# A row softmax on one core: the first loads shared between two DMA queues

## The chip, the cores and the metric

The kernel runs on one core of one Trainium2 chip. The core has a vector engine (VectorE, "DVE" in the profile), a scalar engine (ScalarE, "ACT"), a GpSimd ("POOL") and a Sync engine ("SP") which here only issues DMA transfers. Data move between the device memory and the on-chip memory, which has 128 partitions, by 16 DMA engines. An instruction stream starts a transfer by issuing a DMA on its own queue: Sync's is q1 in the profile, ScalarE's is q10. The metric is the device time of one execution in microseconds (us).

## What is computed

A softmax over the last axis of a float32 array of 16 x 1024 x 512, with temperature 0.5:

```python
temp = 0.5
x_scaled = x / temp
x_max = np.max(x_scaled, axis=-1, keepdims=True)
exp_x = np.exp(x_scaled - x_max)
return (exp_x / np.sum(exp_x, axis=-1, keepdims=True)).astype(np.float32)
```

There are 16,384 rows of 512 numbers: 33.55 MB in and as much out.

## The kernel before

**Tiles.** The 16,384 rows are cut into eight tiles (`c` = 0 to 7). A tile has 128 partitions of `G` = 16 rows each, so 32 KB in a partition and 4.19 MB in all. The 16 rows of a partition follow one another in device memory, so one partition's share is one unbroken piece. Six buffers (`BUFS`) hold tiles 0 to 5; tile 6 takes over the buffer of tile 0, tile 7 that of tile 1, so their loads wait until the stores of tiles 0 and 1 are done.

**Loads.** `load(c)` issues a tile's load on Sync's queue (line 66), all 128 partitions at a time. Tile 0 comes in two parts, four rows of each partition (1 MB) and then twelve (3 MB); the others come whole. Sync has no other work: it runs through its nine issues in order and stops only where a buffer is not free.

**Blocks.** Computation goes by blocks: tile 0 has three (4, 4 and 8 rows of each partition), tiles 1 to 6 have one each, tile 7 has two of 8. So there are eleven blocks, and the loop index `i` counts them. Each passes through these steps, all in place in the tile's buffer:

- `shift(i)`: VectorE takes the negated maximum of each row (line 74, `negmax`) and doubles it (line 78, `bias`).
- `exponentials(i)`: ScalarE computes exp(2x + bias) row by row of each partition and the row's sum with it (line 85), 16 instructions for a full tile.
- `scale_vector(i)`: VectorE takes the reciprocals of the sums (line 100) and multiplies seven eighths of the rows by them (line 102).
- `scale_scalar(i)`: ScalarE multiplies the remaining rows (line 111).
- `store(i)`: at the last block of a tile ScalarE issues the store of the whole tile on its own queue (line 119).

**Order.** The order of instructions is written out by hand (`manual_schedule`), and every engine runs its own in that order. The loop is skewed: in round `i`, ScalarE does the exponentials of block `i+1` before it finishes block `i`, and VectorE scales block `i` and then takes the maximum of block `i+2`. A load is issued in `shift` when a tile is first needed by that order; as Sync waits for nothing but buffers, its first seven issues go out at the start. ScalarE's first instruction of use is a dummy exponential on one column (`warm`, line 52), which brings the load of its function table ahead of the first data.

Of the kernel before, what the change touches and what calls it, by code (L numbers as in the profile page):

```python
# [1 line left out]

# [4 lines left out]


@with_exitstack
def kernel(  # L10
    ctx: ExitStack,
    tc: tile.TileContext,
    x: bass.AP,
    out: bass.AP,
):
    nc = tc.nc
    fp32 = mybir.dt.float32
    P = nc.NUM_PARTITIONS
    AX = mybir.AxisListType.X
    EXP = mybir.ActivationFunctionType.Exp  # L20
    COPY = mybir.ActivationFunctionType.Copy
    MAX = mybir.AluOpType.max

    D = x.shape[-1]
    xf = x.flatten_outer_dims()
    of = out.flatten_outer_dims()
    N = xf.shape[0]

    G = 16
    C = N // (P * G)
    assert C * P * G == N
    xr = xf.rearrange("(c p g) d -> c p g d", p=P, g=G)
    outr = of.rearrange("(c p g) d -> c p g d", p=P, g=G)
    WHOLE = [(0, G)]
    LOADS = [[(0, 4), (4, G)]] + [WHOLE] * 7
    BLOCKS = [[(0, 4), (4, 8), (8, G)]] + [WHOLE] * 6 + [[(0, 8), (8, G)]]
    STORES = [WHOLE] * 8  # L40
    BMAX = 16
    BUFS = 6

    data = ctx.enter_context(tc.tile_pool(name="data", bufs=BUFS))
    stats = ctx.enter_context(tc.tile_pool(name="stats", bufs=6))

    ctx.enter_context(tc.manual_schedule())


    warm = stats.tile([P, 1], fp32, name="warm", bufs=1)  # L50
    nc.vector.memset(warm, 0.0)  # L51
    nc.scalar.activation(out=warm, in_=warm, func=EXP)  # L52

    chunks = {}
    blocks = [(c, lo, hi) for c in range(C) for lo, hi in BLOCKS[c]]
    n = len(blocks)
    biases, sums, recips = {}, {}, {}

    def load(c):
        if c < BUFS:  # L60
            chunks[c] = data.tile([P, G, D], fp32, name="xt")
        else:
            chunks[c] = chunks[c - BUFS]
        xt = chunks[c]
        for lo, hi in LOADS[c]:
            nc.sync.dma_start(out=xt[:, lo:hi, :], in_=xr[c][:, lo:hi, :])  # L66

    def shift(i):
        c, lo, hi = blocks[i]
        if c not in chunks:  # L70
            load(c)
        b = hi - lo
        negmax = stats.tile([P, BMAX], fp32, name="negmax")
        nc.vector.tensor_reduce(  # L74
            negmax[:, 0:b], chunks[c][:, lo:hi, :], axis=AX, op=MAX, negate=True
        )
        biases[i] = stats.tile([P, BMAX], fp32, name="bias")
        nc.vector.tensor_scalar_mul(biases[i][:, 0:b], negmax[:, 0:b], 2.0)  # L78

    def exponentials(i):  # L80
        c, lo, hi = blocks[i]
        sums[i] = stats.tile([P, BMAX], fp32, name="sums")
        for g in range(hi - lo):
            row = chunks[c][:, lo + g, :]
            nc.scalar.activation(  # L85
                out=row,
                in_=row,
                func=EXP,
                bias=biases[i][:, g : g + 1],
                scale=2.0,  # L90
                accum_out=sums[i][:, g : g + 1],
            )


    def scale_vector(i):
        c, lo, hi = blocks[i]
        b = hi - lo
        k = b - b // 8
        recips[i] = stats.tile([P, BMAX], fp32, name="recip")
        nc.vector.reciprocal(recips[i][:, 0:b], sums[i][:, 0:b])  # L100
        rows = chunks[c][:, lo : lo + k, :]
        nc.vector.tensor_mul(  # L102
            rows, rows, recips[i][:, 0:k].unsqueeze(2).broadcast_to((P, k, D))
        )

    def scale_scalar(i):
        c, lo, hi = blocks[i]
        b = hi - lo
        for g in range(b - b // 8, b):
            row = chunks[c][:, lo + g, :]  # L110
            nc.scalar.activation(  # L111
                out=row, in_=row, func=COPY, scale=recips[i][:, g : g + 1]
            )

    def store(i):
        c, _, end = blocks[i]
        for lo, hi in STORES[c]:
            if hi == end:
                nc.scalar.dma_start(
                    out=outr[c][:, lo:hi, :], in_=chunks[c][:, lo:hi, :]  # L120
                )

    shift(0)
    shift(1)
    exponentials(0)
    for i in range(n):
        if i + 1 < n:
            exponentials(i + 1)
        scale_vector(i)
        scale_scalar(i)  # L130
        if i + 2 < n:
            shift(i + 2)
        store(i)


# [1 line left out]
_INS = ['x']  # L137
_OUTS = [((16, 1024, 512), 'float32')]


# [23 lines left out]
```

## Time and profile before

| | |
|---|---|
| Median of three runs | 162.38 us (162.26 to 162.4) |
| The profiled execution's own time | 162.34 us |
| Its span in the profile | 160.6 us |
| Reads and writes of device memory | 33.55 MB and 33.55 MB, 418 GB/s over the span |
| Waits of ScalarE for VectorE's `bias` | 41.2 us in 10 waits, the longest 5.9 |
| Median time of a store from issue to landing | 22.8 us |
| Median time of a whole tile's load from issue to landing | 30.2 us |

The profile's span starts and ends a little inside the device time; 1.74 us lie around it here. A row of the timeline gives the start and the duration in us, the engine, the line of the kernel, the operation, and what it writes and reads with its shape; in brackets stands how long the engine was idle before it and what ended that. "SPq" and "ACTq" are the instructions with which Sync and ScalarE issue transfers. A row of the waits gives who waited for what, the total in us, how often, and the longest. A DMA queue's row gives packets, megabytes, and the time of its packets as a share of 16 engines' span. A row of the windows gives the stretch, its length, the busy time of VectorE, ScalarE and GpSimd in it (with the number of instructions), TensorE's granted clock, the DMA engines' busy share and the GB/s moved.

### The profile page before, as it was taken

Reading aid. Unit: us, or ns where it says so; the run is one execution under the profiler, and the core shown is the slowest. Engines: PE = TensorE matmul, PEld = TensorE weight load, DVE = VectorE, ACT = ScalarE, POOL = GpSimd, SP = SyncE. Lnnn points to the kernel's source line nnn. Section 1 sums busy time; section 2 is a strip of 40 time slices with the busy share of each in tenths; the row PEclk is TensorE's granted clock in tenths of the full one; section 3 lists DMA queues with packets and bytes.
Section 4 is the critical chain, followed back from the end, with each engine's and each line's share of the span. In section 5 each row is a group of like instructions: output and inputs, shape, how many; then the busy total and the mean of one; then the engine's idle time right before and its main releaser. Section 6 shows DMA issues by size and latency. Waiting matters only on the chain.

```text
span 160.6 us, 402 instructions
## 1 busy us (share of the span) xinstructions
DVE 134.6 (84%) x45; ACT 102.1 (64%) x273; POOL 0.2 (0%) x4
## 2 busy tenths in 40 slices
DVE  0507999999999999999999999999999999957000
ACT  3071549069979963998199909991899891790000
POOL 0000000000000000000000000000000000000000
DMA  5999999999999999999999999999999999999993
GB/s 182 471 400 506 400 400 498 408 392 484 424 400 384 400 457 449 400 441 465 400 424 473 408 408 492 400 392 498 416 392 490 424 392 457 457 392 449 465 392 139
DMA packets 2450, 67.13 MB, mean 418 GB/s; under 512 B 272, under 2 KB 272, under 8 KB 272
## 3 DMA queue, kind: packets, MB, share of 16 engines
q1 hardware_dynamic: 1296, 33.56, 49.3%
q10 hardware_dynamic: 1152, 33.55, 48.4%
q14 instruction: 2, 0.02, 0.0%
HBM read 33.55 MB, written 33.55 MB: 418 GB/s over the span
## 4 chain that ended last, share of the span: by engine, by line
DVE 80%; DMA 7%; ACT 4%; issue 0%; SPq 0%
DVE negmax L74 42%; DVE xt L102 36%; DMA xt<-in_x_dram 7%; ACT xt L85 4%; DVE bias L78 1%; DVE recip L100 1%; SPq L66 0%
## 5 line engine op out<-in xcount | busy, mean ns | idle before, releaser
L85 ACT ACTIVATE xt<-xt,bias 128x512 f32<-128x512 f32 x128 | 90.4, 708 | 41.7 <-DVE bias L78 41.2
L74 DVE TENSOR_REDUCE negmax<-xt 128x16 f32<-128x8192 f32 (+2 forms) x11 | 69.9, 6352 | 9.5 <-DMA xt<-in_x_dram 9.5
L102 DVE TENSOR_TENSOR xt<-xt,recip 128x7168 f32<-128x7168 f32 (+2 forms) x11 | 62.0, 5637 | 0.4
L85 ACT ACTIVATION_READ_ACCUMULATOR xt<-xt,bias 128x1 f32 x128 | 23.9, 187 | 0.0
L111 ACT ACTIVATE xt<-xt,recip 128x512 f32<-128x512 f32 x15 | 9.9, 706 | 0.0
L100 DVE RECIPROCAL recip<-sums 128x16 f32<-128x16 f32 (+2 forms) x11 | 2.4, 218 | 1.8 <-ACT xt L85 1.8
L78 DVE TENSOR_SCALAR bias<-negmax 128x16 f32<-128x16 f32 (+2 forms) x11 | 1.9, 173 | 0.4
L52 ACT ACT_TABLE_LOAD x1 | 1.3, 1283 | 0.7 <-PEq L148 0.7
L51 DVE MEMSET warm<- 128x1 f32 x1 | 0.1, 59 | 0.8 <-PEq L148 0.8
L52 ACT ACTIVATE warm<-warm 128x1 f32<-128x1 f32 x1 | 0.2, 203 | 0.0
L148 POOL MEMSET const-bfloat16-1.0<- 128x1 bf16 x1 | 0.1, 103 | 0.0
L148 POOL MEMSET const-uint8-127<- 128x1 uint8 x1 | 0.1, 103 | 0.0
L148 POOL MEMSET const-float32-1.0<- 128x1 f32 x1 | 0.1, 100 | 0.0
L148 POOL MEMSET const-float32-0.0<- 128x1 f32 x1 | 0.1, 99 | 0.2 <-issue 0.2
## 6 DMA issues: line engine op xcount, KB each, us to landing
out_dram<-xt ACTq DMA_DIRECT2D x8, 4096.0 KB, 22.8
xt<-in_x_dram SPq DMA_DIRECT2D x7, 4096.0 KB, 30.2
xt<-in_x_dram SPq DMA_DIRECT2D x1, 3072.0 KB, 11.7
xt<-in_x_dram SPq DMA_DIRECT2D x1, 1024.0 KB, 4.9
```

Source lines behind the costliest of these rows:

```text
L51: nc.vector.memset(warm, 0.0)
L52: nc.scalar.activation(out=warm, in_=warm, func=EXP)
L74: nc.vector.tensor_reduce(negmax[:, 0:b], chunks[c][:, lo:hi, :], axis=AX, op=MAX, negate=True)
L78: nc.vector.tensor_scalar_mul(biases[i][:, 0:b], negmax[:, 0:b], 2.0)
L85: nc.scalar.activation(out=row, in_=row, func=EXP, bias=biases[i][:, g : g + 1], scale=2.0, accum_out=sums[i][:, g : g + 1],)
L100: nc.vector.reciprocal(recips[i][:, 0:b], sums[i][:, 0:b])
L102: nc.vector.tensor_mul(rows, rows, recips[i][:, 0:k].unsqueeze(2).broadcast_to((P, k, D)))
L111: nc.scalar.activation(out=row, in_=row, func=COPY, scale=recips[i][:, g : g + 1])
L148: nc = _bacc.Bacc("TRN2", target_bir_lowering=False, num_devices=1)
```

## The change

Tiles 0, 1 and 2 (`SHARED` = 3) are loaded in two transfers each (tile 0 in two for each of its parts): partitions 0 to 63 on Sync's queue, partitions 64 to 127 on ScalarE's. Tile 3 is loaded whole on ScalarE's queue. Tiles 4 to 7 stay on Sync's queue, whole. The loads of tiles 0 to 2 are issued before anything else; the dummy exponential with its table load comes after them in ScalarE's order. The loads of tiles 3, 4 and 5 are issued after the exponentials of the first block: on ScalarE this places tile 3's load behind those four instructions, while Sync, which has none of them, goes on to tiles 4 and 5 at once. The stores stay on ScalarE's queue, now behind these loads. No computation changes.

```diff
+    SHARED = 3
+
     data = ctx.enter_context(tc.tile_pool(name="data", bufs=BUFS))
     stats = ctx.enter_context(tc.tile_pool(name="stats", bufs=6))
 
     ctx.enter_context(tc.manual_schedule())
-
-
-    warm = stats.tile([P, 1], fp32, name="warm", bufs=1)
-    nc.vector.memset(warm, 0.0)
-    nc.scalar.activation(out=warm, in_=warm, func=EXP)
...
         for lo, hi in LOADS[c]:
-            nc.sync.dma_start(out=xt[:, lo:hi, :], in_=xr[c][:, lo:hi, :])
+            halves = [(nc.sync, 0, P)]
+            if c == SHARED:
+                halves = [(nc.scalar, 0, P)]
+            if c < SHARED:
+                halves = [(nc.sync, 0, P // 2), (nc.scalar, P // 2, P)]
+            for queue, p, q in halves:
+                queue.dma_start(out=xt[p:q, lo:hi, :], in_=xr[c][p:q, lo:hi, :])
...
+    for c in range(SHARED):
+        load(c)
+
+
+    warm = stats.tile([P, 1], fp32, name="warm", bufs=1)
+    nc.vector.memset(warm, 0.0)
+    nc.scalar.activation(out=warm, in_=warm, func=EXP)
+
     shift(0)
     shift(1)
     exponentials(0)
+    for c in range(SHARED, BUFS):
+        load(c)
     for i in range(n):
```

## The prediction

> **What bounds the kernel now.** I read the page first: engine rows, the slices, the DMA queues. Then the waits, the timeline of VectorE and of the two issuing queues, and the windows at the end.
>
> ```profile
> span 160.6 us, 402 instructions
> DVE 134.6 (84%) x45; ACT 102.1 (64%) x273; POOL 0.2 (0%) x4
> ...
> DMA  5999999999999999999999999999999999999993
> ...
> q1 hardware_dynamic: 1296, 33.56, 49.3%
> q10 hardware_dynamic: 1152, 33.55, 48.4%
> ...
> xt<-in_x_dram SPq DMA_DIRECT2D x1, 1024.0 KB, 4.9
> ```
>
> The two data queues, q1 (Sync, loads) and q10 (Scalar, stores), fill 49.3 + 48.4 = 97.7% of the span on all 16 DMA engines: 156.9 us. So 67.1 MB move at 67.13 MB / 156.9 us = 428 GB/s, and one tile of 4.19 MB costs 9.8 us. Only the first and last slice are not full. The transfers are a floor under the whole span.
>
> ```profile
> DVE negmax L74 <- DMA xt<-in_x_dram: 9.5, 2, 4.8
> ...
> SPq L66 <- DMA out_dram<-xt: 75.3, 2, 56.4
> ...
> 5.61 2.29 DVE L74 TENSOR_REDUCE negmax<-xt 128x4 f32<-128x2048 f32 x1 [4.75 <-DMA xt<-in_x_dram]
> 12.88 2.29 DVE L74 TENSOR_REDUCE negmax<-xt 128x4 f32<-128x2048 f32 x1 [4.78 <-DMA xt<-in_x_dram]
> 24.63 8.68 DVE L74 TENSOR_REDUCE negmax<-xt 128x16 f32<-128x8192 f32 x1
> 37.47 8.68 DVE L74 TENSOR_REDUCE negmax<-xt 128x16 f32<-128x8192 f32 x1
> 45.58 0.37 ACTq L119 DMA_DIRECT2D out_dram<-xt  x1
> 54.09 8.68 DVE L74 TENSOR_REDUCE negmax<-xt 128x16 f32<-128x8192 f32 x1
> 69.38 0.33 SPq L66 DMA_DIRECT2D xt<-in_x_dram  x1
> 143.59 3.89 DVE L102 TENSOR_TENSOR xt<-xt,recip 128x3584 f32<-128x3584 f32 x1
> 147.55 0.34 ACTq L119 DMA_DIRECT2D out_dram<-xt  x1
> ...
> 144.00:148.00 4.00, 3.48 (x1) 0.54 (x1) 0.00 (x0) 1.00 0.93 401
> 148.00:152.00 4.00, 0.00 (x0) 0.00 (x0) 0.00 (x0) 1.00 0.91 393
> ```
>
> VectorE waits for data only twice, for the two parts of tile 0 (landed just before 5.61 and 12.88), and then runs without a gap worth naming to 147.48. Tiles 1, 2 and 3 are wanted at 24.63, 37.47 and 54.09. The last store is issued at 147.55 into DMA engines that are still full (0.93, then 0.91), and takes 160.6 - 147.55 = 13.0 us to the end of the span, of which 9.8 are its own bytes. So two things end together: the VectorE chain, and the DMA engines' total work. Anything that adds engine time to the DMA comes out at the end almost one for one; anything that merely shifts VectorE earlier gains next to nothing, because the engines have no spare time to use.
>
> [...] The trace of before agrees with the shared engines (two queues together reach 428 GB/s, each half while both run) but holds no transfer to half the partitions[...].
>
> **The change part by part.**
>
> *Issues moved to Scalar, ahead of the table load.* Sync spends 0.73 to 4.23 on seven issues, 0.5 us each. Scalar will issue four halves first: 4 x 0.5 = 2.0 us, so the table load (1.28) and the warm-up (0.20) end near 0.72 + 2.0 + 1.5 = 4.2. The first exponential starts at 8.13; 3.9 us of cover, cost zero. Without the cover it would cost 2.0.
>
> *Tile 3's load on Scalar after the first exponentials.* They end at 11.06 and ScalarE then stands idle 4.34 us up to 15.40. One issue of 0.5 us lies in that gap. Queued behind it are the next exponentials, which wait for VectorE anyway. Cost zero.
>
> *Waits.* Each reduce of a split load waits on two landings instead of one; the chain's own "issue" pieces are 0.02 us. Four of them: below 0.1 us. Sync's issues of tiles 4 and 5 follow its four halves; a reuse wait on an early landing costs nothing, since neither tile is wanted before 70.
>
> *Order in the rings.* Scalar's ring now holds half of tiles 0 to 2, then tile 3, then the stores; Sync's the other halves, then 4 and 5. At full rate tiles 1 and 2 land as before, 12.86 + 9.8 = 22.7 and 32.5. Tile 3 (Scalar) shares the engines with tile 4 (Sync) and lands at 32.5 + 2 x 9.8 = 52.1 instead of 42.3, wanted at 54.09: 2.0 us of cover. Store 0, issued at 45.58, stands behind it and runs beside tile 5, 52.1 to 71.7; it now lands at 69.38, when Sync issues tile 6. That moves to about 72, tile 6 is then in by about 93 and wanted at 103.94. No cost. The bytes are the same and the engines never run dry, so the order alone leaves the end at 162.3.
>
> *The halves[...].* This is the one part with a price. A tile is 8 packets per engine, 9.8 / 8 = 1.22 us each. [...] Bounds for the 12.6 MB of tiles 0 to 2, 3 x 9.8 = 29.4 us at full rate: nothing[...]; 29.4 us more[...]. Value taken: [...] the share lost is 1 - 0.19 / 1.22 = 0.85: 25.0 us more. All later tiles are whole and pay nothing.
>
> *What is late next.* With 0.85: the second part of tile 0 lands at 12.86 + 0.85 x 9.8 = 21.2, tile 1 at 22.7 + 16.7 = 39.4, tile 2 at 32.5 + 25.0 = 57.5, tiles 3 and 4 together at 77.1. VectorE, which was ready for tile 1 11.75 us after its second reduce (33.0), waits 6.4 there; is ready for tile 2 at 39.4 + 12.84 = 52.2, waits 5.3; ready for tile 3 at 57.5 + 16.62 = 74.1, waits 3.0. That is 23.0 behind its old 54.09; it ends at 170.5, and the last store could end at 170.5 + 13.0 = 183.5. The DMA engines' work, 25.0 longer, ends at 160.6 + 25.0 = 185.6. The later decides.
>
> **Sum.** Profiled execution 162.34 (span 160.6 and 1.74 around it; the median of the runs is 162.38): 162.34 + 25.0 = 187.3. I say 187.
>
> **The rivals.**
>
> *Partial collision.* The start of a queue is ragged (1 MB takes 4.4 us from 1.15 to 5.58, not 2.45)[...]. A loss of a third gives 162.34 + 0.33 x 29.4 = 172.
>
> *No collision, not slower.* [...] Then the order alone counts: 162.3. What may be gained is one parallel issue, 0.37 us: 161.9. For it: the queue rows show no loss when loads and stores alternate, 428 GB/s throughout[...]. It decides once the share lost is below 0.01 (0.3 us).
>
> *Tile 3 late.* If sharing is unequal (Sync's ring served more than half), tile 3 slips beyond its 2.0 us of cover, at most to the end of tiles 4 and 5, 32.5 + 29.4 = 61.9: VectorE 7.8 late. The bytes still flow, so the DMA end doesn't move, but the last store is issued at 155.4 and ends at 168.4: 170. Against it: loads and stores now get equal turns.
>
> **Chances and range.** Collision nearly in step, 178 to 192: 0.55. Partial collision or tile 3 late, 164 to 178: 0.13. No collision: 0.32, of it 0.12 faster, 0.11 within 0.2% (0.3 us, which is what can be told from no change), 0.09 slightly slower. Faster 0.12, same 0.11, slower 0.77. The likeliest case alone spans 178 to 192. A range of the two collision cases alone would miss 0.32, so it reaches down to 162.0; up to 192, which is the full 29.4 on top.
>
> **What would show it.** Right: packets of the halves take up to twice as long, the rate in the slices falls from some 430 to some 230 GB/s until about 57 us and is full after it; VectorE gains waits for tiles 1, 2 and 3; the last stores stand queued. Wrong: the first eight slices keep 400 GB/s and more, tile 2's reduce starts near 37.5. The order step is shown by tile 3 and tile 4 landing together and by no VectorE wait later than tile 3's. If Scalar's first exponential starts later than 0.2 us after its bias, the cover of the issues was wrong.

## The result, and the profile after

The changed kernel takes 189.31 us (median of four runs, 188.74 to 189.71) against 162.39: 1.166 times the time before, 95% interval 1.162 to 1.169. That is 26.9 us more. The profiled execution took 189.71 us, with a span of 187.5.

The page of the changed kernel, engine rows, slices and DMA queues:

```profile
span 187.5 us, 410 instructions
DVE 134.9 (72%) x45; ACT 102.1 (54%) x273; POOL 0.2 (0%) x4
...
DMA  5998999999998999999999999999999999999992
GB/s 136 255 241 199 273 224 224 224 217 217 210 210 281 440 447 440 426 398 419 447 447 440 447 440 419 405 414 447 447 447 447 426 419 412 419 447 447 447 440 126
...
q10 hardware_dynamic: 1616, 44.04, 61.8%
q1 hardware_dynamic: 896, 23.07, 36.0%
```

VectorE and ScalarE do the same work as before, 134.9 and 102.1 us. The DMA engines look as busy as ever in the slices, but up to about 60 us (13 slices of 4.7 us) they move some 200 to 280 GB/s, less in the first, and 398 to 447 after it, the last slice apart. The trap in this page is the busy row: a packet that crawls counts as busy. The two queues' packets now take 61.8 + 36.0 = 97.8% of 187.5 us on 16 engines, 183.4 us where it was 156.9: 26.5 us more for the same 67.13 MB. That is nearly all of the loss of 26.9. The windows of the changed kernel show the rate while the halves of tiles 1 and 2 come in (share and GB/s are the last two columns):

```profile
20.00:40.00 20.00, 11.70 (x8) 8.68 (x24) 0.00 (x0) 1.00 1.05 233
40.00:59.00 19.00, 12.86 (x4) 8.82 (x25) 0.00 (x0) 1.00 0.96 219
```

In the packet records of the trace a 32 KB packet of a half takes 2.37 us (2.34 to 2.39 over tile 1 and tile 2 on both queues), and one of a whole tile 1.21. The records also show the order: 16 packets of Sync's half start within about a microsecond, and 2.4 us later 16 of Scalar's half, in turn until 59 us. That a half uses only some of the DMA engines is not the reason, since the share of all 16 in these windows is 1.05 and 0.96 (the profile's share can come out a little above 1). The timeline of the changed kernel shows who waited (the row maximum is on line 78 here, the loads on line 70):

```profile
3.61 1.28 ACT L133 ACT_TABLE_LOAD   x1 [3.61 <-issue]
8.15 2.29 DVE L78 TENSOR_REDUCE negmax<-xt 128x4 f32<-128x2048 f32 x1 [7.29 <-DMA xt<-in_x_dram]
10.68 0.72 ACT L89 ACTIVATE xt<-xt,bias 128x512 f32<-128x512 f32 x1 [5.57 <-DVE bias L82]
10.70 0.36 ACTq L70 DMA_DIRECT2D xt<-in_x_dram  x1
22.31 2.29 DVE L78 TENSOR_REDUCE negmax<-xt 128x4 f32<-128x2048 f32 x1 [11.67 <-DMA xt<-in_x_dram]
41.25 8.69 DVE L78 TENSOR_REDUCE negmax<-xt 128x16 f32<-128x8192 f32 x1 [7.11 <-DMA xt<-in_x_dram]
60.41 8.69 DVE L78 TENSOR_REDUCE negmax<-xt 128x16 f32<-128x8192 f32 x1 [6.24 <-DMA xt<-in_x_dram]
79.69 8.69 DVE L78 TENSOR_REDUCE negmax<-xt 128x16 f32<-128x8192 f32 x1 [2.58 <-DMA xt<-in_x_dram]
173.17 0.34 ACTq L123 DMA_DIRECT2D out_dram<-xt  x1
```

VectorE waits for every load up to tile 3 and for none after it. The last store is issued at 173.17 and takes 14.3 us to the end of the span, 1.3 more than before: it stands behind a backlog, since the packets of the store before it run until 176.2, 3.1 us past the issue, where it was 2.1 us in the kernel before. So the DMA engines' total work sets the end, ahead of VectorE by that little.

### The profile page after: what moved, and what is told of

It is laid out like the page before. It is cut to its first block, busy times and chain, and to the rows that moved or that the text cites. A ratio compares the mean times of both kernels' runs of the same rounds, so it can differ in the third digit from the quotient of the medians.

```text
span 187.5 us, 410 instructions
## 1 busy us (share of the span) xinstructions
DVE 134.9 (72%) x45; ACT 102.1 (54%) x273; POOL 0.2 (0%) x4
## 2 busy tenths in 40 slices
DMA packets 2514, 67.13 MB, mean 358 GB/s; under 512 B 336, under 2 KB 336, under 8 KB 336
## 3 DMA queue, kind: packets, MB, share of 16 engines
q10 hardware_dynamic: 1616, 44.04, 61.8%
## 4 chain that ended last, share of the span: by engine, by line
DVE 62%; DMA 21%; another core or an unknown queue 5%; ACT 3%; ACTq 1%; issue 0%; DVEq 0%
DVE negmax L78 32%; DVE xt L106 29%; DMA xt<-in_x_dram 21%; ACT xt L89 3%; ACTq L70 1%; DVE bias L82 1%; DVE recip L104 1%; DVEq L78 0%
## 6 DMA issues: line engine op xcount, KB each, us to landing
out_dram<-xt ACTq DMA_DIRECT2D x8, 4096.0 KB, 26.5
```

## The experiments

Three readings of the slow packets were set against each other: that it matters which partitions a transfer touches, that two queues of loads ("two rings" in what was expected) hinder each other, and that a half tile's reads collide in memory. Where a run tells them apart, the first number expected is for the first of them. Beside them stands the question what the new order of the loads does.

**Whole tiles, new order.** Only the halves are taken out of the change.

```diff
-                halves = [(nc.sync, 0, P // 2), (nc.scalar, P // 2, P)]
+                halves = [(nc.sync, 0, P)]
```

> Keeps everything of the change but the halves: tiles 0 to 2 go whole on Sync, tile 3 whole on Scalar, the table load behind them. [...] 162.4 within 0.5, all of the 26.9 us gone. Order (tile 3 ahead of the stores, late table load): it keeps the loss, 185 or more.

Measured: 168.96 us, 1.041 times before (1.040 to 1.042). Neither number: 20 us are gone, 6.6 stay. The timeline of this run shows why:

```profile
8.09 0.38 ACTq L70 DMA_DIRECT2D xt<-in_x_dram  x1
...
32.26 8.69 DVE L78 TENSOR_REDUCE negmax<-xt 128x16 f32<-128x8192 f32 x1 [6.38 <-DMA xt<-in_x_dram]
```

Tile 3's load went out at 8.09, beside the first exponential and not behind all four. Scalar's queue was empty, so tile 3, wanted last, took turns with the rest of tile 0 and with tile 1 (its packets run from 12.0 to 29.4 us, tile 1's from 14.5 to 31.8), and VectorE got tile 1 at 32.26 instead of 24.63. The experiment had changed more than it meant to: without the halves nothing holds tile 3 back. A later run put tile 3 on Sync too:

```diff
-            if c == SHARED:
-                halves = [(nc.scalar, 0, P)]
```

> The run with whole tiles (169.0) with tile 3 on Sync too, so that Scalar carries stores only. If its 6.6 us came from tile 3 being issued on an empty Scalar queue at 8.1, ahead of tiles 1 and 2: 162.4 within 0.4, and no VectorE wait for tile 1. If something else of the order did it: 165 or more.

Measured: 162.30 us, ratio 0.9997 (0.9988 to 1.0006). VectorE waits only for the two parts of tile 0 again. The 6.6 us were tile 3's early place; with all loads on Sync, placing their issues earlier in the program costs nothing.

**Half the rows instead of half the partitions.** Both queues still carry half of each tile.

```diff
-            halves = [(nc.sync, 0, P)]
+            mid = (lo + hi) // 2
+            halves = [(nc.sync, lo, hi)]
             if c == SHARED:
-                halves = [(nc.scalar, 0, P)]
+                halves = [(nc.scalar, lo, hi)]
             if c < SHARED:
-                halves = [(nc.sync, 0, P // 2), (nc.scalar, P // 2, P)]
-            for queue, p, q in halves:
-                queue.dma_start(out=xt[p:q, lo:hi, :], in_=xr[c][p:q, lo:hi, :])
+                halves = [(nc.sync, lo, mid), (nc.scalar, mid, hi)]
+            for queue, a, b in halves:
+                queue.dma_start(out=xt[:, a:b, :], in_=xr[c][:, a:b, :])
```

> Both queues still carry half of each of tiles 0 to 2, but half the rows of all 128 partitions in place of all rows of 64. [...] 162.4 within 1, packets at about 27 GB/s per engine. Two rings (loads alternating between two queues hinder one another): about 189, as after the change. Addresses (half a tile lies in 2 MB of memory and its reads collide there): 162 to 163, since each transfer again spans the whole tile.

Measured: 164.31 us, 1.012 (1.010 to 1.013), a little beyond the forecast. Two queues of loads side by side are not slow: 25.0 of the 26.9 us are gone. For the 1.9 left, tile 3 was put on Sync in this kernel as well:

> As the run with half the rows on each queue (164.3), but tile 3 whole on Sync, so that nothing stands ahead of the first store on Scalar. If the 1.9 us left there come from tile 3's place on Scalar (store 0 later, Sync's ring dry before tile 6): 162.4 within 0.4. If they come from cutting the tiles by rows (smaller packets, later first landing): 164.3 within 0.4.

Measured: 162.73 us, 1.003 (1.002 to 1.004). So some 1.6 us belong to tile 3's place on Scalar, and 0.4 to the cut and the issues. The queue rows of the two runs, with tile 3 on Scalar first:

```profile
q10 hardware_dynamic: 1872, 44.04, 63.2%
q1 hardware_dynamic: 1152, 23.07, 34.3%
```

```profile
q10 hardware_dynamic: 1728, 39.85, 57.5%
q1 hardware_dynamic: 1296, 27.26, 40.1%
```

That is 97.5% of a span of 162.5, 158.4 us of engine time, against 97.6% of 161.0, 157.1. So 1.3 of the 1.5 us between these two executions are slower packets, not idle engines. In the packet records 1.05 of them lie in tile 6, whose load starts on a Sync queue that had been dry since 70.8 us (packets up to 2.58 us). That a dry queue alone slows them is not shown: in the changed kernel Sync's queue is dry before tile 6 too, from 97.2 to 102.7 us, and its packets there take 1.21. The reason stays open.

**Both halves on one queue.**

```diff
-                halves = [(nc.sync, 0, P // 2), (nc.scalar, P // 2, P)]
+                halves = [(nc.sync, 0, P // 2), (nc.sync, P // 2, P)]
```

> The same halves of partitions, both on Sync's queue, one after the other, no second ring. [...] 189 to 192[...]. Two rings: 162.4. Addresses: 189.

Measured: 198.51 us, 1.222 (1.220 to 1.225). The second queue is not needed for the loss. The slices of this run (4.9 us each):

```profile
GB/s 130 244 225 202 314 307 287 321 214 214 214 214 214 214 215 427 427 428 427 428 434 448 427 454 441 454 434 429 427 428 428 427 220 427 427 428 427 214 427 214
```

From slice 10 to 15 only halves move, at 214 GB/s, half of the 427 and 428 that stand in most slices from 16 on. In slices 5 to 9 tile 3, again early on an empty Scalar queue, is mixed in. The run lies 6.5 us above the forecast's upper end. VectorE waits 16.2 us for the second part of tile 0, the DMA engines' work is 187.8 us ((49.5 + 46.2)% of 196.2), 4.4 more than in the changed kernel, and near the end the engines twice stand idle for about 2 us. That tile 3's early place is behind all of this is likely, but no run shows it.

**Other addresses.** The halves read interleaved 32 KB pieces, so that each spans the whole tile in memory.

```diff
+    xs = xf.rearrange("(c p h g) d -> c h p g d", p=P // 2, h=2, g=G)
...
-                queue.dma_start(out=xt[p:q, lo:hi, :], in_=xr[c][p:q, lo:hi, :])
+                src = xr[c][p:q, lo:hi, :]
+                if c < SHARED:
+                    src = xs[c][p // 64][:, lo:hi, :]
+                queue.dma_start(out=xt[p:q, lo:hi, :], in_=src)
```

> The changed kernel with another source for the halves of tiles 0 to 2: partitions 0 to 63 read every even 32 KB piece of the tile in memory, 64 to 127 every odd one, so that each half transfer spans the tile's whole 4.19 MB; the rows of these tiles come out in another order. [...] 189 within 1.5, packets of the halves at 2.4 us. Addresses (a half's 2 MB of memory collide): back to 162 to 165.

Measured: 189.12 us, 1.165 (1.162 to 1.168), the changed kernel's time, with packets of the halves at 2.35 us. Spread over twice the memory the halves are as slow as before, so colliding addresses are not what slows them.

**Which 64 partitions.** The first try gave Sync partitions 32 to 95 of tiles 1 and 2, and Scalar the two outer quarters.

```diff
-            if c < SHARED:
-                halves = [(nc.sync, 0, P // 2), (nc.scalar, P // 2, P)]
+            if 0 < c < SHARED:
+                halves = [(nc.sync, 32, 96), (nc.scalar, 0, 32), (nc.scalar, 96, P)]
```

> Tile 0 whole; of tiles 1 and 2 Sync carries partitions 32 to 95[...], Scalar 0 to 31 and 96 to 127[...]. [...] Sync's packets of these tiles at full rate, 1.2 us, Scalar's at 2.4; half of a two-tile loss, 9.8 us, so about 172. Size alone (64 partitions are slow wherever they lie) or addresses: all packets slow, 2 x 9.3 = 18.6 more, about 181.

Measured: 193.26 us, 1.190 (1.182 to 1.198), far from both. The time is not usable for the question, since Scalar's four slow quarters started at once and held up tile 0. In the waits of this run it shows as two waits of VectorE, 42.3 us together:

```profile
DVE negmax L78 <- DMA xt<-in_x_dram: 42.3, 2, 24.5
```

The packets do answer it: those of Sync's middle partitions took 1.22 us at the mean, those of Scalar's quarters 2.58. They did not run beside one another, though: the quarters ended at 33.4 us, and the middle parts came from 43.7 on.

The cleaner form edits only tile 2 of the kernel before, all on Sync. First two plain halves:

```diff
-            nc.sync.dma_start(out=xt[:, lo:hi, :], in_=xr[c][:, lo:hi, :])
+            parts = [(0, 64), (64, P)] if c == 2 else [(0, P)]
+            for p, q in parts:
+                nc.sync.dma_start(out=xt[p:q, lo:hi, :], in_=xr[c][p:q, lo:hi, :])
```

> The kernel before with one edit: tile 2's load is cut into partitions 0 to 63 and 64 to 127, both on Sync. [...] 8 packets per engine at twice 1.21 us, 9.7 us more, so 172.1 within 1, and 215 to 220 GB/s while they run (about 22.6 to 42). Step-keeping of two rings needed: 162.4, since there is one ring only.

Measured: 175.24 us, 1.080 (1.078 to 1.081). Then the same with the middle first:

```diff
-            parts = [(0, 64), (64, P)] if c == 2 else [(0, P)]
+            parts = [(32, 96), (0, 32), (96, P)] if c == 2 else [(0, P)]
```

> The kernel before with tile 2's load cut into partitions 32 to 95, then 0 to 31, then 96 to 127, all on Sync. [...] the middle half[...], at full rate, the two quarters at half rate: 4.8 us more, 167.2 within 1, and some 430 GB/s for the first 4.9 us of the tile, 215 to 220 for the 9.7 after. Size (64 partitions or fewer are slow wherever they lie): 172 or more.

Measured: 168.28 us, 1.037 (1.036 to 1.039), 0.1 beyond the forecast's upper end. The windows in which tile 2 comes in, of the run with two halves:

```profile
21.00:32.00 11.00, 10.93 (x5) 5.75 (x16) 0.00 (x0) 1.00 1.06 226
...
32.00:43.00 11.00, 5.39 (x4) 9.53 (x27) 0.00 (x0) 1.00 0.91 203
```

of the kernel before in the same stretches:

```profile
21.00:32.00 11.00, 10.93 (x5) 5.75 (x16) 0.00 (x0) 1.00 0.99 429
...
32.00:43.00 11.00, 10.93 (x5) 9.45 (x27) 0.00 (x0) 1.00 0.99 427
```

and of the run with the middle half and two quarters:

```profile
21.50:26.50 5.00, 4.93 (x5) 4.18 (x12) 0.00 (x0) 1.00 0.97 419
27.00:36.50 9.50, 9.43 (x4) 4.04 (x13) 0.00 (x0) 1.00 0.95 210
```

This decides it. Sixty-four partitions from 32 to 95 come in at 419 GB/s, 64 from 0 to 63 or from 64 to 127 at 203 to 226, and the two quarters of 32 at 210. It is not how many partitions, but which. What makes the difference inside the chip is not shown by any trace.

The total of the first run, 12.9 us, is 3.2 more than the forecast, although its queues took (51.2 + 44.8)% of 173.6 = 166.7 us, 9.8 more than before, as forecast. Its timeline has the rest (the row maximum is on line 76 here):

```profile
95.21 8.69 DVE L76 TENSOR_REDUCE negmax<-xt 128x16 f32<-128x8192 f32 x1 [1.86 <-DMA xt<-in_x_dram]
115.25 8.69 DVE L76 TENSOR_REDUCE negmax<-xt 128x16 f32<-128x8192 f32 x1 [3.33 <-DMA xt<-in_x_dram]
134.60 4.42 DVE L76 TENSOR_REDUCE negmax<-xt 128x8 f32<-128x4096 f32 x1 [2.63 <-DMA xt<-in_x_dram]
```

Once stores run, loads get every second turn: in the packet records of the kernel before, between 58 and 66 us, 16 packets of Sync and 16 of Scalar start in turn, 1.21 us each, and tile 5's packets take 18.9 us beside stores where tile 1's take 10.2 alone. The loads, 9.8 us behind when the stores begin, finish about twice that later: tile 7, which landed at 115.1 before, landed at 134.6. Its slack of 5.4 us (wanted at 120.56) is used up, VectorE is 14.0 late, and the engines stand idle before the last store (2.9 us, in the packet records). The run with the middle half has less of the same: its queues took 4.8 us more than before, as forecast, and the last tile came late there too.

**Tile 3's place in the changed kernel.** The same two lines taken out of the changed kernel, halves kept.

> The changed kernel with tile 3 whole on Sync instead of Scalar. If tile 3's place on Scalar costs nothing in the changed kernel (the prediction): 189.3 within 0.7. If it costs 1.6 as in the runs with half the rows: 187.7. If it helps, because it holds the stores back while loads are late (tile 2 in halves alone cost 12.9, 3 more than its bytes): later loads then share the engines with stores and land late, 190.5 or more, with new VectorE waits after 100.

Measured: 193.24 us, 1.191 (1.188 to 1.194): 3.9 us slower than the changed kernel. Its first store's packets start at 66.2 us, not at 79.4. Its timeline has the late waits again:

```profile
112.69 8.69 DVE L76 TENSOR_REDUCE negmax<-xt 128x16 f32<-128x8192 f32 x1 [1.77 <-DMA xt<-in_x_dram]
132.71 8.69 DVE L76 TENSOR_REDUCE negmax<-xt 128x16 f32<-128x8192 f32 x1 [3.31 <-DMA xt<-in_x_dram]
152.05 4.42 DVE L76 TENSOR_REDUCE negmax<-xt 128x8 f32<-128x4096 f32 x1 [2.63 <-DMA xt<-in_x_dram]
```

So tile 3 ahead of the stores is a help where the loads are late, since it keeps the stores out of their way; where they are on time, with the tiles cut by rows, it costs 1.6 us.

**Beside stores, and in the other direction.** Tile 6 in halves, in the kernel before (`c == 6` in place of `c == 2`):

> The kernel before with tile 6's load, which runs beside stores (about 74 to 93), cut into partitions 0 to 63 and 64 to 127. [...] its 8 packets per engine pay double there too, 9.7 us more DMA time at the end, 172 within 1.5. [...] 162.4 to 167.

Measured: 170.13 us, 1.049 (1.043 to 1.054), between the two. The packets of the halves took 1.99 and 2.11 us at the mean, where those of the changed kernel took 2.37, and the store packets beside them 1.37, where they take 1.21 in the kernel before. That makes 6.7 and 1.3 us, which accounts for the 7.9 us of the run. Why the halves lose less beside stores is not shown. Tile 4's store in halves asks whether moving data out of half the partitions is as slow as moving it in:

```diff
-                nc.scalar.dma_start(
-                    out=outr[c][:, lo:hi, :], in_=chunks[c][:, lo:hi, :]
-                )
+                parts = [(0, 64), (64, P)] if c == 4 else [(0, P)]
+                for p, q in parts:
+                    nc.scalar.dma_start(
+                        out=outr[c][p:q, lo:hi, :], in_=chunks[c][p:q, lo:hi, :]
+                    )
```

> The kernel before with tile 4's store (about 119 to 130, no load beside it) cut into partitions 0 to 63 and 64 to 127. [...] 9.7 us more, 172 within 1.5. If only writing into it is limited so: 162.4.

Measured: 172.91 us, 1.066 (1.054 to 1.077). Windows of this run while the halved store goes out:

```profile
126.00:130.00 4.00, 4.00 (x1) 4.00 (x11) 0.00 (x0) 1.00 0.88 221
130.00:134.00 4.00, 4.00 (x2) 2.94 (x8) 0.00 (x0) 1.00 1.00 221
```

A store out of 64 partitions from 0 or from 64, at 221 GB/s, is as slow as a load into them, at 203 to 226. Its packets are less even, at 1.21 to 3.50 us.

## Why the prediction was right, step by step

- **The halves** are what costs, as forecast. The price is engine time (183.4 against 156.9 us), it appears with one queue (198.51 us) as with two (189.31), it stayed with other addresses (189.12), and it is absent where the 64 partitions are those from 32 to 95 (419 GB/s). Two halves at once get hardly more than one after the other: 219 to 233 GB/s on two queues, 203 to 226 on one, where whole tiles get 427. That halves would be slow was my estimate, which nothing in the trace of before showed, and why they are slow is not shown by these runs either.
- **The size** was a little low: 25.0 forecast, 26.9 measured. The mis-sized term is the share lost. The 0.85 was my estimate, from a guess of 0.19 us that no trace shows; the packets of 2.37 us, where whole tiles have 1.21, give 0.96. That the sum came so close is partly luck. With 0.96 it would be some 28 us for three tiles. Tiles 1 and 2 do lose 9.3 us each in the packet records, but tile 0 only 8.2, 1.6 of it in its first part and 6.6 in its second. The range, 162.0 to 192, spans every case that was named, so lying in it says little; the packets and the landings say more.
- **The landings** follow from it. Forecast and found by VectorE: second part of tile 0, 21.2 and 22.3; tile 1, 39.4 and 41.2; tile 2, 57.5 and 60.4; tile 3, 77.1 and 79.7. Tiles 3 and 4 landed together, 79.5 and 79.7, and no VectorE wait for a load came after.
- **That the DMA work decides the end** held, by the backlog of 1.3 us; VectorE alone was 25.6 us behind (173.17 against 147.55).
- **Scalar's issues** took 2.85 us, not 2.0, since a half's issue costs 0.58 to 0.84 us. The table load and warm-up ended at 5.1. The cover held: the first exponential starts at 10.68, as soon as its bias is there.
- **Tile 3's issue** I placed behind the first exponentials, at 11. It went out at 10.70, beside the first of them. Harmless here, since its bytes stood behind Scalar's halves (its packets start at 59.98); 6.6 us in the run where they did not. Sync's issues of tiles 4 and 5 did not go out at once either, but at 5.78 and 22.31, each just after a landing of tile 0 (5.76 and 22.29); neither tile was wanted before 96.
- **"The order alone leaves the end at 162.3"** was the step that failed. In the kernel with half the rows the same order costs 1.6 us, and under late loads it gains 3.9. I had checked each landing against its need, tile 6 behind store 0 too, but took it that the engines never run dry and keep their full rate. With tile 3 on Scalar, tile 6's packets slow down in the kernel with half the rows (up to 2.58 us). And under late loads I had not counted what the stores take from the loads by their turns. The sum for the changed kernel was hardly touched by it: tile 3 does hold the stores back there, and the 3.9 us show only when it is moved away.
- **The rivals.** No packet of tiles 1 and 2 took less than 2.34 us, so neither the loss of a third nor the case without loss took place. Tile 3 was not served unequally, as it landed with tile 4.

No version here beats the kernel before. With 97.7% of its span filled by packets at full rate, a second queue has nothing to add.

## What to carry to other kernels

A busy DMA row is not a full DMA row (a share of 1.05 moved 233 GB/s here, one of 0.99 moved 429 in the kernel before): read the GB/s beside it, and where it halves, ask which partitions the transfer touches. To share a tile between queues, cut it along the free axis and leave all 128 partitions in each part (164.31 us here, against 189.31); if partitions must be cut, a part from 32 to 95 kept the full rate here, 419 GB/s, one from 0 to 63 did not, 226. Before a load is moved to another queue, ask what it will take turns with: an empty queue serves a late tile early, at the cost of those that are wanted first (6.6 us here), and a load ahead of stores may help (3.9 us here, where loads were late) or hurt (1.6, where they were on time).

## What was not expected of the hardware

- The slow packets of the halves do not recover in 39 us (tiles 1 and 2): they stay at 2.34 to 2.39 us, just short of twice 1.21. In one queue they were even a little slower (2.47 and 2.51 us in the two halves of tile 2), more than twice; what adds to them is not known.
- Stores from half the partitions fall to 221 GB/s too.
- Tile 3's load, behind four exponentials in ScalarE's stream, was issued while they still ran (0.02 us after the start of the first one, in the changed kernel and in the run with whole tiles). This load had nothing to wait for.
- Of tile 0's first part, Sync's half landed at 5.8 us and Scalar's, issued at the same moment (0.73), at 8.1: the first packets of the two queues did not take turns (Sync's start at 2.05 us, Scalar's at 4.07). In the run with half the rows they landed together, at 5.7 and 5.9.
